# Norm offset parts on GpSimd behind the rotary tables' copies, and one row's attention norm offset on VectorE

## The chip, the cores and the metric

The kernel runs on one core of a Trainium2 chip, as one launch. The core's engines each work through their own fixed list of instructions: TensorE (PE in the profile, with PEld for the loading of weights), VectorE (DVE), ScalarE (ACT), GpSimd (POOL) and SyncE (SP, which only starts transfers here). Transfers are also started from GpSimd's list. An instruction waits at the head of its list until what it reads is there, and everything behind it on that engine waits too. The metric is device time in microseconds (us); lower is better.

## The reference

A decoder trunk of two layers over 1024 tokens of width 1024, all in float32. What matters here is the first layer's mixer and the norm behind it:

```
h = x @ w_in                                  # split: c_q (256), k, v (128 each), k_idx (128), w_idx (8)
k = apply_rope(k, cos_q, sin_q)               # 2 heads of 64, the first 16 elements rotate
k_idx = apply_rope(layer_norm(k_idx, g, b), cos_i, sin_i)     # the first 32 of 128 rotate
q, q_idx = apply_rope(c_q @ w_uq), apply_rope(c_q @ w_iq)
score = sum over 8 heads of w_idx * relu(q_idx . k_idx); keep the 256 best keys of each query
h = layer_norm(alpha * x + attention(q, k, v) @ w_o, ln_g, ln_b)
ffn = (silu(h @ w_gate) * (h @ w_up)) @ w_down
h = layer_norm(alpha * h + ffn, ...)          # and the same again with a gated recurrence as the mixer
```

`cos` and `sin` come from the positions; `layer_norm` is `(x - mean) * rsqrt(var + eps) * g + b`, and `b` is what is called the norm's offset below.

## The kernel before, in words

The 1024 tokens are 8 rows of 128 tokens (one row is 128 partitions x 1024 values; row 7 is the last). Every float32 product is made of three TensorE matmuls on a high and a low part of each operand (`mm3`, lines 110 to 112); ScalarE makes the high part by a cast, VectorE the low part by a subtraction.

**Attention's projections** (`att_in`). The steps in `ORDER_IN` are called one by one: `p0` projects row 0 with `w_in`, `f2` turns row 2 into feature order, `k0` makes the keys of rows 0 and 1, `w` splits the query weights, `q2` makes the queries of row 2, `s2` stores them, `a` advances the index scores. A scheduler then sets the order on each engine from the order of the calls and from what depends on what; the result is a fixed list for each engine.

Three things in this part matter here.

- **Rotary tables** (`rope_tables`). VectorE reduces the angles; ScalarE takes the sine twice (line 206, once for the cosine with a shift of a quarter turn); behind each sine GpSimd copies the table into a second half (line 207) and into a short table for the 64-wide heads (line 209, twice). `keys` (from line 1308) reads the short tables in its first rotary multiplication (line 221, tile `rk`). What follows there: two sums (lines 224, 225), ScalarE's split of the keys (line 1328, tile `kk`), and TensorE's transposes of the keys (line 1343).
- **Offset parts** (`kits`). For the later norms that are folded into matmuls, GpSimd prepares the offsets of two norms, each plain (`o...`) and multiplied by alpha (`p...`): a small 4-row tile `za` is loaded from memory (line 396), combined (lines 399 to 401), and split into three bfloat16 parts (lines 404, 408), each written back to memory (line 405). Before these, a 0/1 selector is made from the identity (line 388) and written three times (line 390). `kits` is a generator: each `next` emits one stretch of this work. Its results are read by `picks` and `parts` in the later down projections.
- **Index loads** (line 1441). While queries are stored, GpSimd's list also starts the loads of stored index queries (tile `it`), which TensorE multiplies with the index keys (tile `C`, from `kih`). On GpSimd's list they stand behind all of `kits`.

**The end of attention** (`att_main`). Rows 0 to 5 are normed while the last queries are attended; rows 6 and 7 at the very end by `layer_norm((6, 7), ...)`. For each row VectorE subtracts the mean and multiplies by the gain (line 151), ScalarE multiplies by the inverse deviation (line 152), and GpSimd adds the offset in two halves of 512 (line 154). The feed-forward's operands are then made of pairs of rows, (0, 2), (1, 3), (4, 6), (5, 7): `row_sums` subtracts rows of a pair (lines 374, 375, tile `gb`; on VectorE for the last two pairs), TensorE transposes rows and differences (line 352, tile `Y`), ScalarE and VectorE split them (lines 471, 472, tile `x`), and TensorE multiplies them with the first weights (tile `M`).

The calls at the point of the change are:

```
kits = self.kits(ap, self.tile(s.sel, [P, T], F32, "za"), s.bs)
for step in self.ORDER_IN.split():
    next(kits, None)
    does[step[0]](int(step[1:] or 0))
```

Of the kernel before, what the change touches and what calls it, by code (L numbers as in the profile page):

```python
# [18 lines left out]
ALU = mybir.AluOpType  # L19
# [48 lines left out]
class Core:  # L68
# [66 lines left out]
    def layer_norm(self, ts, g, b):  # L135

        nc, v = self.nc, self.nc.vector
        n = len(ts)
        mv = self.tile(self.small, [P, 4, 2], F32, "lnmv")[:, :n]
        for i, t in enumerate(ts):  # L140
            r = self.resid[:, t, :]
            st = self.tile(self.small, [P, 2, 6], F32, "lnst")
            for c in range(2):
                v.bn_stats(st[:, c, :], r[:, c * 512 : (c + 1) * 512])
            v.bn_aggr(mv[:, i, :], st.rearrange("p a b -> p (a b)"))
            yield
        rs = self.rsqrt(mv[:, :, 1], n, 1.0, LN_EPS, "ln")
        yield
        for i, t in enumerate(ts):
            r = self.resid[:, t, :]  # L150
            v.scalar_tensor_tensor(r, r, mv[:, i, 0:1], g, op0=ALU.subtract, op1=ALU.mult)
            nc.scalar.activation(r, r, AF.Copy, scale=rs[:, i : i + 1])
            for c in (slice(0, 512), slice(512, D)):
                nc.gpsimd.tensor_tensor(r[:, c], r[:, c], b[:, c], op=ALU.add)
            yield

    def row(self):
# [10 lines left out]
    def rope_tables(self, cp, wp, pt, it):  # L168

        nc, v = self.nc, self.nc.vector  # L170
        n = NT * 16
        pf = self.tile(wp, [P, NT], F32, "posf")
        v.tensor_copy(pf, pt)
        three = self.tile(wp, [P, 3, n], F32, "kk")
        ang, a1, a2 = (three[:, i, :] for i in range(3))
        v.tensor_tensor(
            ang.rearrange("p (t j) -> p t j", t=NT),
            pf.rearrange("p (t o) -> p t o", o=1).to_broadcast([P, NT, 16]),
            it.rearrange("p (o j) -> p o j", o=1).to_broadcast([P, NT, 16]),
            op=ALU.mult,  # L180
        )
        v.tensor_copy(a1.bitcast(F32R), ang)
        v.tensor_tensor(a2, ang, a1, op=ALU.subtract)
        turns = self.tile(wp, [P, 7, n], F32, "q")
        near = self.tile(wp, [P, 7, n], F32, "qi")
        for i, (a, p) in enumerate(((a1, 3), (a2, 2), (a1, 2), (a2, 1), (a1, 1), (a2, 0), (a1, 0))):
            v.tensor_scalar(turns[:, i, :], a, TURN[p], None, op0=ALU.mult)

        def frac(x, tmp, magic):
            v.tensor_scalar(tmp, x, magic, magic, op0=ALU.add, op1=ALU.subtract)  # L190
            v.tensor_tensor(x, x, tmp, op=ALU.subtract)

        frac(turns, near, 1.5 * 2.0**35)
        frac(turns, near, 1.5 * 2.0**23)
        u = turns[:, 0, :]
        for i in range(1, 7):
            v.tensor_tensor(u, u, turns[:, i, :], op=ALU.add)
        tabs = []
        for i, off in enumerate((0.25, 0.0)):
            w = turns[:, 1 + i, :]  # L200
            v.tensor_scalar(w, u, off, None, op0=ALU.add)
            frac(w, near[:, 0, :], 1.5 * 2.0**23)
            v.tensor_scalar(w, w, -0.4999999, 0.4999999, op0=ALU.max, op1=ALU.min)
            o, e = (self.tile(cp, [P, NT, 2, n], F32, f"rope{i}{n}") for n in (16, 8))
            w = w.rearrange("p (t j) -> p t j", t=NT)
            nc.scalar.activation(o[:, :, 0, :], w, AF.Sin, scale=2.0 * math.pi)
            nc.gpsimd.tensor_copy(o[:, :, 1, :], o[:, :, 0, :])
            for j in range(2):
                nc.gpsimd.tensor_copy(e[:, :, j, :], o[:, :, 0, 0:16:2])
            tabs.append((o, e))  # L210
        return zip(*tabs)

# [165 lines left out]
    def kits(self, pool, work, bs):  # L378

        nc, gp = self.nc, self.nc.gpsimd
        self.select = self.tile(self.kd, [12, 512], BF16, "select")
        self.kit = {}
        y = work[0:4, 0:256].bitcast(BF16)
        ones = self.ident[0:4, 0:4].rearrange("p (k o) -> p k o", o=1).to_broadcast([4, 4, P])
        gp.tensor_copy(y.rearrange("p (k c) -> p k c", k=4), ones)
        for j in range(3):
            gp.dma_start(self.select[4 * j : 4 * j + 4], y)  # L390
        yield
        rest, part = work[0:4, 0:512], work[0:4, 512:1024].bitcast(BF16)
        four = rest.rearrange("k (i c) -> k i c", i=4)
        for b, name, scale in bs:
            o = self.kit[name] = self.tile(self.kd, [12, 512], BF16, self.name(name[0]))
            gp.dma_start(four[:, 0:2, :], b.rearrange("(i k c) -> k i c", i=2, k=4))
            yield
            if scale is not None:
                gp.tensor_scalar(four[:, 0:2, :], four[:, 0:2, :], scale, None, op0=ALU.mult)
            gp.tensor_tensor(four[:, 2, :], four[:, 0, :], four[:, 1, :], op=ALU.subtract)  # L400
            gp.tensor_scalar(four[:, 3, :], four[:, 1, :], -1.0, None, op0=ALU.mult)
            for j in range(3):
                x = part[:, j % 2 * 512 : (j % 2 + 1) * 512]
                gp.tensor_copy(x, rest)
                gp.dma_start(o[4 * j : 4 * j + 4], x)
                yield
                if j < 2:
                    gp.tensor_tensor(rest, rest, x, op=ALU.subtract)
# [809 lines left out]
    def att_in(self, ap, csp, tp, x):  # L1218
        nc, v, gp, s = self.nc, self.nc.vector, self.nc.gpsimd, self.att
# [199 lines left out]

        does = dict(p=project, f=feature, k=keys, q=query, s=store, w=lambda _: query_weights(), a=lambda _: advance())  # L1420
        kits = self.kits(ap, self.tile(s.sel, [P, T], F32, "za"), s.bs)
        for step in self.ORDER_IN.split():
            next(kits, None)
            does[step[0]](int(step[1:] or 0))

    @staticmethod
# [608 lines left out]
```

## Time and profile before

| what | value |
|---|---|
| median of 3 runs | 2513.41 us (2510.82 to 2516.71) |
| the profiled execution | 2517.95 us |
| its span, first to last instruction | 2516.2 us |
| mean granted TensorE clock | 0.989 |
| TensorE busy | 2441.9 us |
| VectorE busy | 1906.9 us |
| ScalarE busy | 1056.2 us |
| GpSimd busy | 176.9 us |

The prediction quotes rows of the profile. A row of the timeline reads: start and duration in us, engine, line, operation, what is written from what, shapes, how many of a kind, and in brackets the engine's idle time ahead of it with what ended it. A row of the waits reads: engine, tile and line that waited, `<-` what it waited for: us in total, times, longest. A row of the windows reads: from and to, length, then busy time and number of instructions for PE, PEld, DVE, ACT and POOL, the granted TensorE clock as a share of full speed, the busy share of the transfer engines, and GB/s. A matmul of 128x384 has a moving operand of 384 columns. All times in rows are counted from the span's start.

### The profile page before, as it was taken

What the parts mean: (1) busy time and instruction counts of PE and PEld (TensorE: products, weight loads), DVE (VectorE), ACT (ScalarE), POOL (GpSimd) and SP (SyncE); (2) the same over time, 40 slices, a digit from 0 to 9 for tenths busy, and PEclk for the clock granted to TensorE, in tenths of its full rate; (3) what the DMA queues carried; (4) which work ended last, traced back from release to release, by engine and by line L of the source; (5) the groups of instructions that cost most, each with busy time, mean ns of one, the idle gap of its engine ahead of it and who ended that gap; (6) DMA issues with size and microseconds to landing.
All of it is one profiled execution on the core that took longest, in us unless ns stands there. A gap on an engine that the chain in (4) does not pass through costs nothing.

```text
span 2516.2 us, 35546 instructions
## 1 busy us (share of the span) xinstructions
PE 2441.9 (97%) x12810; PEld 2041.3 (81%) x12810; DVE 1906.9 (76%) x3692; ACT 1056.2 (42%) x1972; POOL 176.9 (7%) x295
## 2 busy tenths in 40 slices
PE   6998999999999999999999999999999999999998
PEld 6887888888888888888788888887778888888886
DVE  6578776788997766566898888887889867665767
ACT  4467666564333333334443333333353333333431
POOL 6001002000000000000011111111000000000000
PEclk8998999999999999999999999999999999999999
DMA  3337001011895332665431111113638733326853
GB/s 133 109 125 240 26 22 56 18 47 71 291 328 176 94 120 92 236 217 195 144 104 47 55 43 55 43 55 110 230 122 293 267 101 93 121 92 235 281 183 117
DMA packets 140127, 338.94 MB, mean 135 GB/s; under 512 B 17288, under 2 KB 18088, under 8 KB 132264
## 3 DMA queue, kind: packets, MB, share of 16 engines
q1 hardware_dynamic: 137224, 329.19, 38.6%
q0 software_dynamic: 2720, 7.42, 1.0%
q8 instruction: 101, 1.65, 0.3%
q14 instruction: 82, 0.67, 0.1%
HBM read 232.15 MB, written 104.39 MB: 134 GB/s over the span
## 4 chain that ended last, share of the span: by engine, by line
PE 64%; issue 10%; DVE 5%; DMA 2%; ACT 1%; POOL 1%; SPq 0%; DVEq 0%; ACTq 0%; POOLq 0%
PE Y L112 11%; PE Y L110 11%; PE Y L111 11%; PE M L111 8%; PE M L112 8%; PE M L110 7%; PE M L1082 3%; PE M L352 1%; DVE w L472 1%; DMA raw<-in_wd_dram 1%; PE M L1067 1%; PE M L1144 1%; PE M L1131 1%; PE M L1146 1%; PE M L354 0%
## 5 line engine op out<-in xcount | busy, mean ns | idle before, releaser
L471 ACT CAST w<-raw 128x512 fp32r<-128x512 f32 (+1 forms) x373 | 288.3, 775 | 527.7 <-PE Y L112 273.8
L472 DVE TENSOR_TENSOR w<-raw,w 128x512 fp32r<-128x512 f32 (+1 forms) x373 | 327.1, 881 | 180.8 <-ACT w L471 178.6
L110 PE MATMUL Y<-x,w 128*128 128x512 f32 (+1 forms) x1120 | 433.2, 387 | 1.8 <-DVE rows L789 0.7
L111 PE MATMUL Y<-x,w 128*128 128x512 f32 (+1 forms) x1120 | 429.9, 384 | 0.0
L112 PE MATMUL Y<-x,w 128*128 128x512 f32 (+1 forms) x1120 | 428.1, 382 | 0.0
L111 PE MATMUL M<-x,w 128*128 128x512 f32 (+1 forms) x644 | 245.7, 382 | 3.3 <-DVE x L472 3.3
L110 PE MATMUL M<-x,w 128*128 128x512 f32 (+1 forms) x644 | 245.6, 381 | 0.1
L110 PEld LDWEIGHTS Y<-x,w 128*128 128x128 f32 x1120 | 211.8, 189 | 41.3 <-ACT w L471 1.2
L112 PE MATMUL M<-x,w 128*128 128x512 f32 (+1 forms) x644 | 245.2, 381 | 0.0
L112 PEld LDWEIGHTS Y<-x,w 128*128 128x128 f32 x1120 | 211.8, 189 | 39.2 <-issue 0.9
L111 PEld LDWEIGHTS Y<-x,w 128*128 128x128 f32 x1120 | 211.9, 189 | 37.1 <-issue 0.2
L471 ACT CAST w<-s 128x512 fp32r<-128x512 f32 x180 | 111.8, 621 | 303.6 <-PE Y L112 116.5
L472 DVE TENSOR_TENSOR w<-s,w 128x512 fp32r<-128x512 f32 x180 | 124.4, 691 | 52.0 <-ACT w L471 51.1
L111 PEld LDWEIGHTS M<-x,w 128*128 128x128 f32 x644 | 121.6, 189 | 26.6 <-DVE x L472 3.7
L110 PEld LDWEIGHTS M<-x,w 128*128 128x128 f32 x644 | 121.5, 189 | 24.3 <-ACT x L471 1.2
L112 PEld LDWEIGHTS M<-x,w 128*128 128x128 f32 x644 | 121.6, 189 | 22.8
L110 PE MATMUL Y<-w 128*128 128x512 f32 x284 | 111.8, 394 | 0.2 <-ACT ph L471 0.2
L111 PE MATMUL Y<-w,w 128*128 128x512 f32 x284 | 111.4, 392 | 0.1
L112 PE MATMUL Y<-w,w 128*128 128x512 f32 x284 | 111.4, 392 | 0.0
L111 PE MATMUL M<-w,w 128*128 128x512 f32 x248 | 97.0, 391 | 1.3 <-DVE w L472 1.3
L112 PE MATMUL M<-w,w 128*128 128x512 f32 x248 | 96.9, 391 | 0.0
L110 PE MATMUL M<-w 128*128 128x512 f32 x248 | 96.1, 391 | 0.2 <-ACT ph L471 0.2
(497 smaller groups left out, 5112.4 us busy)
## 6 DMA issues: line engine op xcount, KB each, us to landing
raw<-in_wgu_dram SPq DMA_DIRECT2D x44, 1024.0 KB, 6.1
wdt<-in_wd_dram SPq DMA_DIRECT2D x44, 512.0 KB, 5.2
raw<-in_wd_dram SPq DMA_DIRECT2D x66, 256.0 KB, 4.2
raw<-in_hw_dram SPq DMA_DIRECT2D x16, 1024.0 KB, 4.8
qd<-qx SPq DMA_DIRECT2D x16, 512.0 KB, 3.6
qt<-qd SPq DMA_DIRECT2D x64, 128.0 KB, 2.7
t5q<-wdt SPq DMA_DIRECT2D x26, 256.0 KB, 3.7
t7q<-wdt SPq DMA_DIRECT2D x26, 256.0 KB, 2.7
```

Of the source, the lines that this page charges most:

```text
L110: mm(out, a[0], b[0], start=first, stop=False, **kw)
L111: mm(out, a[0], b[1], start=False, stop=False, **kw)
L112: mm(out, a[1], b[0], start=False, stop=last, **kw)
L352: mm(y[:, c], x[:, c], self.ident, **flags)
L471: self.nc.scalar.copy(hi, x)
L472: ins = (eng or self.nc.vector).tensor_tensor(lo, x, hi.bitcast(F32), op=ALU.subtract)
L1067: nc.tensor.matmul(pl[:, n, :], kk[:, m : m + P], y[:, n, :], start=True, stop=True)
L1082: nc.tensor.matmul(pl[rows, n, cols], lhs, rhs, start=True, stop=True)
L1131: nc.tensor.matmul(pd[:, n, :], kt[:, n, :], vt[:, n, :], start=True, stop=True)
L1144: nc.tensor.matmul(po[:, n, :], at[:, n, :], vt[:, n, :], start=True, stop=states[n] is None)
L1146: nc.tensor.matmul(po[:, n, :], qd[:, n * P : (n + 1) * P], states[n], start=False, stop=True)
```

## The change

Three edits.

- The `kits` generator is not advanced during the first six steps (`p0 f2 p1 f3 k0 w`); it starts at the seventh, `p2`.
- Its first instruction, the cast that makes the selector, gets an order-only dependence on the last copy of the rotary tables: on GpSimd's list it may not stand ahead of it.
- In `layer_norm` the two halves of row 7's offset are added by VectorE. Rows 6 and 7 are normed together by one call, and only attention's norm goes through this function; the other rows stay on GpSimd.

```diff
@@ layer_norm
             for c in (slice(0, 512), slice(512, D)):
-                nc.gpsimd.tensor_tensor(r[:, c], r[:, c], b[:, c], op=ALU.add)
+                (v if t == 7 else nc.gpsimd).tensor_tensor(r[:, c], r[:, c], b[:, c], op=ALU.add)
@@ rope_tables
             for j in range(2):
-                nc.gpsimd.tensor_copy(e[:, :, j, :], o[:, :, 0, 0:16:2])
+                self.roped = nc.gpsimd.tensor_copy(e[:, :, j, :], o[:, :, 0, 0:16:2])
@@ kits
-        gp.tensor_copy(y.rearrange("p (k c) -> p k c", k=4), ones)
+        self.behind(gp.tensor_copy(y.rearrange("p (k c) -> p k c", k=4), ones), self.roped)
@@ att_in
-        for step in self.ORDER_IN.split():
-            next(kits, None)
+        for i, step in enumerate(self.ORDER_IN.split()):
+            if i > 5:
+                next(kits, None)
             does[step[0]](int(step[1:] or 0))
```

`behind` adds a dependence that sets the order on the engine's list and no wait.

**GpSimd's list near the start.** Before, the tables' copies (tile `rope`; 76 and 77 belong to the cosine, 78 and 79 to the sine) stand inside the third offset, `o_131`:

```order
L396 DMA za_292<-in_lnb_dram 4x2x128
L400 TENSOR_TENSOR za_292<-za_292 4x128
L401 TENSOR_SCALAR za_292<-za_292 4x128
L404 CAST za_292<-za_292 4x512
L405 DMA o_131_682<-za_292 4x512
L207 COPY rope_76_276<-rope_76_276 128x8x16
L209 COPY rope_77_277<-rope_76_276 128x8x8 x2
L408 TENSOR_TENSOR za_292<-za_292 4x512
L404 CAST za_292<-za_292 4x512
L405 DMA o_131_682<-za_292 4x512
```

and the sine's copies six rows further on. With the change (line numbers from 1423 on are one higher):

```order
L1502 TENSOR_SCALAR marks_129<-marks_129 128x1
L1662 MEMSET bias_13_85 128x256
L1664 AFFINE_SELECT bias_14_86<-bias_14_86 128x128
L1664 AFFINE_SELECT bias_13_85<-bias_13_85 128x128
L207 COPY rope_76_276<-rope_76_276 128x8x16
L209 COPY rope_77_277<-rope_76_276 128x8x8 x2
L207 COPY rope_78_286<-rope_78_286 128x8x16
L209 COPY rope_79_287<-rope_78_286 128x8x8 x2
L388 CAST za_292<-ident 4x512
L390 DMA select_527<-za_292 4x512 x3
L396 DMA za_292<-in_lnb_dram 4x2x128
L400 TENSOR_TENSOR za_292<-za_292 4x128
```

All copies now stand ahead of the selector and the four offsets; the index loads of line 1441 still stand behind the last offset.

**VectorE's list at the end of attention.** Before, the pair sums (`gb_10624` for rows 4 and 6, `gb_10627` for rows 5 and 7) and the operands' low parts (tile `x`, from transposes in `Y`) stand so:

```order
L509 TENSOR_TENSOR raw_10412<-raw_10412,M_10516 128x256
L374 TENSOR_TENSOR gb_10624<-resid_2201 128x512
L375 TENSOR_TENSOR gb_10624<-gb_10624,resid_2201 128x512
L472 TENSOR_TENSOR x_1619_10380<-Y_10562,x_1619_10380 128x4x128
L374 TENSOR_TENSOR gb_10627<-resid_2201 128x512
L472 TENSOR_TENSOR x_1619_10380<-Y_10569,x_1619_10380 128x4x128
L472 TENSOR_TENSOR x_1620_10381<-Y_10589,x_1620_10381 128x4x128
L375 TENSOR_TENSOR gb_10627<-gb_10627,resid_2201 128x512
```

and with the change:

```order
L509 TENSOR_TENSOR raw_10412<-raw_10412,M_10516 128x256
L374 TENSOR_TENSOR gb_10624<-resid_2201 128x512
L154 TENSOR_TENSOR resid_2201<-resid_2201,gb_2236 128x512 x2
L472 TENSOR_TENSOR x_1619_10380<-Y_10562,x_1619_10380 128x4x128
L472 TENSOR_TENSOR x_1619_10380<-Y_10569,x_1619_10380 128x4x128
L375 TENSOR_TENSOR gb_10624<-gb_10624,resid_2201 128x512
L472 TENSOR_TENSOR x_1620_10381<-Y_10589,x_1620_10381 128x4x128
L374 TENSOR_TENSOR gb_10627<-resid_2201 128x512
L509 TENSOR_TENSOR raw_10412<-raw_10412,M_10445 128x256
L375 TENSOR_TENSOR gb_10627<-gb_10627,resid_2201 128x512
```

The second low part of `x_1619` moves ahead of both sums that follow the offset, and row 7's offset stands between the first sum and the first low part. On ScalarE's and SyncE's lists nothing moves; on TensorE's list one matmul of 128x256 passes the first four transposes of the sums.

## The prediction

> **What bounds the kernel now.** I read the page's busy shares first, then the waits of TensorE, then the windows around its longest wait. The rows are: the page's TensorE share, three of its waits (up to 640 us), and two windows.
>
> ```profile
> PE 2441.9 (97%) x12810; PEld 2041.3 (81%) x12810; DVE 1906.9 (76%) x3692; ACT 1056.2 (42%) x1972; POOL 176.9 (7%) x295
> ...
> PE C L1343 <- ACT kk L1328: 15.9, 1, 15.9
> ...
> PE C L110 <- DMA it<-id: 5.0, 4, 1.8
> PE M L111 <- DVE x L472: 3.3, 1, 3.3
> ...
> 40.00:50.00 10.00, 0.00 (x0) 0.00 (x0) 0.00 (x0) 0.00 (x0) 7.75 (x15) 0.51 0.01 2
> 50.00:60.00 10.00, 7.04 (x34) 6.76 (x35) 7.64 (x27) 3.38 (x11) 7.71 (x14) 0.64 0.01 1
> ```
>
> TensorE is busy for 97% of the span, and every list is fixed, so what TensorE idles is what can be won: an idle stretch that disappears moves everything behind it forward. The largest single one is 15.9 us, and in the window 40 to 50 only GpSimd works, while the transfer engines are at 0.01. This stall has one cause at a time, which the timeline around it shows, engine by engine:
>
> ```profile
> 36.07 0.33 PE L111 MATMUL A<-winl,xsh 128*128 128x384 f32 x1
> ...
> 38.82 0.31 ACT L206 ACTIVATE rope<-q 128x128 f32<-128x128 f32 x1 [3.95 <-DVE q L203]
> ...
> 39.81 0.16 DVE L123 SCALAR_TENSOR_TENSOR aiy<-ait,aiy 128x4 f32<-128x4 f32 x1
> ...
> 49.84 0.28 POOL L207 COPY rope<-rope 128x128 f32<-128x128 f32 x1
> 50.08 0.41 POOL L209 COPY rope<-rope 128x64 f32<-128x64 f32 x2
> ...
> 50.52 0.23 DVE L221 TENSOR_TENSOR rk<-hc,rope 128x64 f32<-128x64 f32 x1 [10.55 <-POOL rope L209]
> ...
> 51.56 0.71 ACT L1328 CAST kk<-hc 128x256 fp32r<-128x256 f32 x2 [12.11 <-DVE aiy L123]
> ...
> 52.33 1.97 PE L1343 MATMUL C<-ident,kk 128*128 128x128 f32 x8 [15.93 <-ACT kk L1328]
> ```
>
> The second sine is there at 39.13, its copies run only at 49.84 to 50.49, because they stand behind offset work on GpSimd's list. VectorE waits 10.55 us at its first rotary multiplication, and from that multiplication to the transposes of the keys it is another 1.8 us.
>
> **The change part by part. First term: the copies move ahead.** Were nothing else different, the copies (0.65 us) would end at 39.13 + 0.65 = 39.8 and the stall would shrink by 50.5 - 39.8 = 10.7 us. But the offset work also goes away from the stretch before the sine, and there it slows VectorE:
>
> ```profile
> 21.08 1.48 DVE L190 TENSOR_SCALAR qi<-q 128x896 f32<-128x896 f32 x1
> ...
> 24.50 0.61 DVE L190 TENSOR_SCALAR qi<-q 128x896 f32<-128x896 f32 x1
> ...
> 33.35 0.21 DVE L203 TENSOR_SCALAR q<-q 128x128 f32<-128x128 f32 x1
> ...
> 33.62 1.12 DVE L119 TENSOR_SCALAR aiy<-aih 128x4 int32<-128x4 int32 x1
> ...
> 37.62 1.17 DVE L203 TENSOR_SCALAR q<-q 128x128 f32<-128x128 f32 x1
> ...
> 66.39 0.16 DVE L119 TENSOR_SCALAR aiy<-aih 128x4 int32<-128x4 int32 x1
> ...
> 31.83 1.05 ACT L1256 CAST w_iqh<-sc 128x1024 fp32r<-128x1024 f32 x1 [1.70 <-DMA sc<-in_w_iq_dram]
> ...
> 34.41 0.46 ACT L1303 COPY hc<-A 128x384 f32<-128x384 f32 x1
> ```
>
> The same instruction on the same shape takes 1.48 or 0.61, 1.17 or 0.21, 1.12 or 0.16 us: 0.87 + 0.96 + 0.96 = 2.8 us too long in three instructions, and the long ones lie where GpSimd computes. So the sine could start at 38.82 - 2.8 = 36.0. With smaller stretches it may be earlier still, but not before ScalarE has ended its copy, 34.41 + 0.46 = 34.9, and that copy stands behind a cast that itself waited for a load, so GpSimd has no hand in it. I take 35.4, in the middle. Sine 0.3, copies 0.65: 36.4. The selector's cast now starts right behind the copies and may hold VectorE's multiplication for up to its 0.6 us (row below); half of that gives 36.7. Gain 50.5 - 36.7 = **13.8 us**. The lower end: VectorE stays as slow as it is, and the cast holds it fully, 10.7 - 0.6 = 10.1. The upper end: sine at 34.9, no hold, multiplication at 35.9, gain 14.6. TensorE is still busy to 36.4, so about 2 us of its idle time remain.
>
> **Second term: the clock behind the stall.** In the window 50 to 60 TensorE worked 7.04 us at a granted clock of 0.64. At full clock that is 4.5 us, 2.5 less. With a gap of 2 instead of 15.9 us the clock may stay up, but the transposes there also wait for VectorE's key chain, so I take **1.5**, with ends 0 and 2.5. The Trainium skill (TensorE: Matmul & The Clock Gate, Part 1) says that the clock is halved after an idle window of some 3.4 us, and restored after as long a busy one. By that rule a gap of 2 us costs no clock and the term is at its upper end. The two windows agree as far as the long gap goes (0.51, then 0.64); no row here has a gap of 2 us.
>
> **Third term: the offsets run later, beside other work.** All offset work of GpSimd, some 50 us, now starts at 36.7. What is queued behind it are the index loads:
>
> ```profile
> 2.71 0.60 POOL L388 CAST za<-ident 4x512 bf16<-4x512 f32 x1 [0.92 <-DMA ident<-in_ident_dram]
> ...
> 11.03 0.66 POOL L396 DMA_DIRECT2D za<-in_lnb_dram  x1 [4.53 <-DMA select<-za]
> ...
> 23.87 0.65 POOL L396 DMA_DIRECT2D za<-in_lnb_dram  x1
> ...
> 40.21 0.65 POOL L396 DMA_DIRECT2D za<-in_lnb_dram  x1
> ...
> 50.97 0.65 POOL L396 DMA_DIRECT2D za<-in_lnb_dram  x1
> ...
> 61.95 0.54 POOL L405 DMA_DIRECT2D p<-za  x1 [0.29 <-POOL za L404]
> ...
> 99.17 1.12 POOL L1441 DMA_DIRECT2D it<-id  x2 [36.68 <-DMA id<-qx]
> ...
> 109.32 0.42 PE L110 MATMUL C<-kih,it 128*128 128x384 f32 x1
> ...
> DMA to landing us min/median/max: 3.1/3.9/5.2
> ```
>
> The four offsets begin at 11.03, 23.87, 40.21 and 50.97, and the last ends at 62.5: 12.8, 16.3, 10.8 (9.5 without the two groups of copies) and 11.5 us; the selector takes 8.3 at most. The first two ran while VectorE was full and transfers dense, the last two while both were calmer, as they are from 37 on. So 2 x (9.5 + 11.5) plus about 5 for the selector, an estimate from these rows, is 47 us: the end at 83.7. TensorE first needs an index load at 109.3 - 15.3 = 94.0, and the load takes two issues and a median of 3.9 us, about 4.5: it must be issued by 89.5. There are 6 us to spare, so the wait costs nothing. What it does cost is VectorE's stretch in its key and query work from 62 us on, which was free of GpSimd:
>
> ```profile
> 57.37 1.00 DVE L221 TENSOR_TENSOR rk<-hc,rope 128x64 f32<-128x64 f32 x1
> ...
> 59.47 0.23 DVE L221 TENSOR_TENSOR rk<-hc,rope 128x64 f32<-128x64 f32 x1
> ```
>
> One rotary multiplication is 0.8 us longer beside GpSimd. Four or five such, each hidden in TensorE's queue for the most part, I price at **-1.0**, with ends 0 and -4 (five of 0.8 all on the path).
>
> **Fourth term: row 7's offset on VectorE.**
>
> ```profile
> 598.77 2.19 ACT L152 ACTIVATE resid<-resid,lny 128x1024 f32<-128x1024 f32 x2
> ...
> 600.00 2.53 POOL L154 TENSOR_TENSOR resid<-resid,gb 128x512 f32<-128x512 f32 x2 [74.52 <-ACT resid L152]
> ...
> 604.17 1.71 POOL L154 TENSOR_TENSOR resid<-resid,gb 128x512 f32<-128x512 f32 x1
> ...
> 601.34 1.75 DVE L374 TENSOR_TENSOR gb<-resid 128x512 f32<-128x512 f32 x1 [0.87 <-POOL resid L154]
> ...
> 605.92 0.69 DVE L374 TENSOR_TENSOR gb<-resid 128x512 f32<-128x512 f32 x1 [0.56 <-POOL resid L154]
> 606.53 0.68 DVE L472 TENSOR_TENSOR x<-Y,x 128x512 fp32r<-128x512 f32 x1
> ...
> 607.27 0.58 PE L111 MATMUL M<-x,w 128*128 128x256 f32 x1 [3.33 <-DVE x L472]
> ```
>
> TensorE stands for 3.33 us at an operand whose low part is queued behind the second pair's sum, and that sum waits for row 7's offset, which GpSimd ends at 605.88. With the change GpSimd is done with row 6 at 602.53. The first sum still runs against GpSimd's second half and ends at 603.1. Then VectorE: two halves of row 7 (ScalarE was ready at 600.96) and two low parts, four instructions 0.61 apart (as 605.92 and 606.53 are): 605.5. TensorE continues at 605.6 instead of 607.27: **1.7 us**. If the halves took GpSimd's 1.27 us each, only 0.4 would be left; if the first sum were not slowed, 2.8. The Trainium skill (SBUF — State Buffer, section "SBUF: two separate sides") calls the port pair of VectorE and GpSimd an exclusive lock, so that the loser waits for the whole instruction. The rows agree: the first sum ends 0.56 us behind the end of GpSimd's second half, and GpSimd's last half takes 1.71 instead of 1.27. The same rule speaks against the third term, since each offset instruction may then stop a rotary one; by it that term would be near its lower end.
>
> **Fifth term:** with the gap at 1.7 instead of 3.3 us the clock may stay up; I take **0.5**, ends 0 and 1.1 (the same share of the gap's 3.33 as 2.5 would be at most of 7.04).
>
> Sum: 13.8 + 1.5 - 1.0 + 1.7 + 0.5 = 16.5 us. Against its own time, the profiled execution of 2517.95 us (span 2516.2 and 1.75 around it) goes to 2501.5. That execution was 4.5 above the median of the runs; from the median, 2513.41 - 16.5 = **2497**. The ends of the terms, added: 10.1 + 0 - 4 + 0.4 + 0 = 6.5 and 14.6 + 2.5 + 0 + 2.8 + 1.1 = 21.0, thus 2492 to 2507.
>
> **The rivals.**
>
> *VectorE was not slowed by GpSimd.* The long rows above could have other causes, and the sine stays at 38.8. Then only the 10.1 of the first term holds: 16.5 - 3.7 = 12.8, time 2500.6. For it: the profile names no cause of a long instruction. Against it: equal instructions come out up to seven times apart in length, and the short L119 lies where GpSimd is idle. Chance 0.23.
>
> *The index loads become the wait.* If all four offsets take as long as the first two, 8.3 + 2 x (12.8 + 16.3) = 66.5, they end at 103.2, 13.7 us behind what TensorE needs; 2.8 us of the gain remain, time 2510.6. For it: the queue is in order, and the third term's stretch slows GpSimd too. Against it: the transfers are idle there (0.01 in two windows). Chance 0.03.
>
> *The same, further: slower.* All of the gain is gone when the offsets take 89.5 + 16.5 - 36.7 = 69.3 us; from there each us is a loss. If every offset took the longest, 16.3, it would be 73.5 us, 4.2 us too many: 2517.6. For it: GpSimd and VectorE now collide in the rotary work of the keys and queries. Against it: it asks for the slowest offset four times. Chance 0.03.
>
> *The gain is given back.* TensorE already waits 5.0 us for index loads; if transfers further on were paced by something other than the lists, the first three terms would vanish and 2.2 remain: 2511.2. Against it: no wait here hangs on a fixed time. Chance 0.03. That the copies do not move is ruled out by the lists; that they move and still wait is the first rival.
>
> **How the numbers follow.** My forecast has 0.68, the rivals 0.23, 0.03, 0.03 and 0.03. The range takes in the forecast's ends and the first rival, widened by some 2 us on the lower side for the spread of the runs shown (2510.82 to 2516.71) and by 1 above: 2490 to 2508. What a measurement of this kernel can tell from no change is about 0.2%, 5 us: faster means below 2508.4. Faster: 0.68 + 0.23 = 0.91; within 0.2%: 0.03 + 0.03 = 0.06; slower: 0.03.
>
> **What would show it.** Right: the wait of TensorE's key transposes falls from 15.9 to about 2 us, the second sine starts near 35.4, the rows 21.08 and 33.62 come back at 0.61 and 0.16, the window behind the stall has a clock near 1, the offsets end near 84 and the first index loads wait for the stored queries, not for GpSimd. At the end of attention TensorE's wait is near 1.7 us. Wrong: a sine still near 38.8 (first rival), index loads issued right behind an offset's last write (second and third), or a stall as short as forecast, with the start of the feed-forward part not earlier by about 17 us (fourth).

## The result, and the profile after

| | before | after |
|---|---|---|
| median | 2513.41 us (2510.82 to 2518.57, 5 runs) | 2498.80 us (2497.97 to 2501.23, 5 runs) |
| profiled execution | 2517.95 us, span 2516.2 | 2497.97 us, span 2496.2 |
| mean granted TensorE clock | 0.989 | 0.995 |

The ratio is 0.9941, with a 95% interval of 0.9926 to 0.9957: 14.8 us faster, between 10.8 and 18.6. The two profiled executions differ by 20.0 us, because that of before lay 4.5 above its median and that of after 0.8 below its own.

The page's busy shares of after, and TensorE's waits:

```profile
PE 2434.2 (98%) x12810; PEld 2033.9 (81%) x12810; DVE 1909.5 (76%) x3694; ACT 1057.1 (42%) x1972; POOL 171.6 (7%) x293
```

```profile
PE C L110 <- DMA it<-id: 4.6, 4, 1.8
...
PE B L1396 <- DVE qx L230: 3.3, 1, 3.3
...
PE C L1343 <- ACT kk L1328: 2.4, 1, 2.4
...
PE M L111 <- DVE x L472: 1.6, 1, 1.6
PE C L1354 <- DVE hc L225: 1.6, 1, 1.6
...
PE C L1343 <- DVE xsl L230: 0.8, 1, 0.8
```

The wait at the key transposes fell from 15.9 to 2.4 us and that at row 7 from 3.3 to 1.6. Three waits on VectorE are new or longer: 0.8 at the transposes of the second keys, 1.6 at the sums `hc` behind them, 3.3 at the queries' low part `qx` (before had two there, the longer one 1.2). The stretch behind the stall, in windows:

```profile
40.00:50.00 10.00, 9.41 (x67) 8.37 (x65) 9.15 (x28) 6.23 (x17) 6.52 (x10) 1.00 0.22 66
50.00:60.00 10.00, 7.91 (x56) 7.37 (x57) 8.59 (x26) 2.50 (x7) 7.13 (x11) 1.00 0.12 46
...
80.00:90.00 10.00, 6.65 (x37) 6.23 (x36) 8.07 (x20) 2.15 (x4) 4.75 (x8) 0.83 0.29 111
```

Where before stood still from 40 to 50 and ran at a clock of 0.64 from 50 to 60, TensorE now works at full clock. From 80 to 90 it idles for 3.35 us and its clock is 0.83; in before the same work lies some 11 us later, and from 90 to 100 TensorE there has 9.65 us of work and a clock of 1.00.

The timeline around the tables (VectorE's once long instructions, the sine, the selector's cast, the first rotary multiplication, the key transposes):

```profile
20.62 0.63 DVE L190 TENSOR_SCALAR qi<-q 128x896 f32<-128x896 f32 x1
...
32.83 0.17 DVE L119 TENSOR_SCALAR aiy<-aih 128x4 int32<-128x4 int32 x1
...
35.44 0.22 DVE L203 TENSOR_SCALAR q<-q 128x128 f32<-128x128 f32 x1
...
35.70 0.31 ACT L206 ACTIVATE rope<-q 128x128 f32<-128x128 f32 x1 [0.55 <-DVE q L203]
...
36.73 0.60 POOL L388 CAST za<-ident 4x512 bf16<-4x512 f32 x1
36.82 0.60 DVE L221 TENSOR_TENSOR rk<-hc,rope 128x64 f32<-128x64 f32 x1 [0.18 <-POOL rope L209]
...
39.00 1.15 PE L1343 MATMUL C<-ident,kk 128*128 128x128 f32 x8 [2.44 <-ACT kk L1328]
```

The three VectorE instructions that took 1.48, 1.12 and 1.17 us before take 0.63, 0.17 and 0.22. The sine starts at 35.70 and the multiplication at 36.82, where the selector's cast holds it (0.60 instead of the 0.23 of before).

**Where the gain arises and where it is lost.** The two lists of TensorE hold the same 12810 matmuls, so each can be followed: the table gives by how much the same instruction starts earlier than in the profile of before.

| TensorE instruction (its start before) | change | change again |
|---|---|---|
| key transposes (52.33) | 13.3 | 14.3 |
| next key transposes, L1354 (59.52) | 16.0 | 15.7 |
| L1354 of the second keys (72.55) | 13.8 | 13.6 |
| query transposes, L1396 (96.30) | 10.8 | 10.5 |
| first index product (109.32) | 10.8 | 10.4 |
| at 300 | 13.6 | 10.7 |
| ahead of the wait at row 7 (600.1) | 13.7 | 10.8 |
| behind that wait (607.27) | 15.4 | 12.5 |
| at 613 | 16.1 | 13.2 |
| at 1000 | 16.1 | 11.2 |
| last | 20.0 | 14.0 |

The right column is a second profile of the same kernel. Up to the index products the two agree within 1 us; from 300 to 613 they stand 3 us apart, at 1000 it is 5, and at the end 6. So up to the index products and across row 7 the columns tell something, and a difference of a few us late in the span does not. Much of this drift can be the clock: the second profile has 41.4 us at half clock, the first 27.4 (before 58.0), and if TensorE worked through all of the 14.0 us between them, they cost 7.0 us (an estimate). Both lose 5.2 or 5.3 us between the second and the fourth line. The rows of that stretch, GpSimd's and VectorE's side by side:

```profile
47.15 0.69 POOL L404 CAST za<-za 4x512 bf16<-4x512 f32 x1
...
47.29 0.68 DVE L230 TENSOR_TENSOR xsl<-C,xsh 128x512 fp32r<-128x512 f32 x1
...
57.40 1.14 POOL L408 TENSOR_TENSOR za<-za 4x512 f32<-4x512 f32 x1
57.44 1.15 DVE L225 TENSOR_TENSOR hc<-hc,rk 128x32 f32<-128x32 f32 x1
...
58.73 0.41 PE L1354 MATMUL C<-ident,hc 128*128 128x128 f32 x2 [1.58 <-DVE hc L225]
...
78.83 1.23 POOL L408 TENSOR_TENSOR za<-za 4x512 f32<-4x512 f32 x1
78.97 1.39 DVE L221 TENSOR_TENSOR rq<-xin,rope 128x256 f32<-128x256 f32 x1
...
81.66 1.19 POOL L408 TENSOR_TENSOR za<-za 4x512 f32<-4x512 f32 x1
81.76 1.24 DVE L225 TENSOR_TENSOR xin<-xin,rq 128x128 f32<-128x128 f32 x1
...
83.80 0.54 POOL L405 DMA_DIRECT2D p<-za  x1 [0.29 <-POOL za L404]
85.51 1.12 PE L1396 MATMUL B<-ident,q 128*128 128x128 f32 x4 [3.35 <-DVE qx L230]
88.39 1.13 POOL L1442 DMA_DIRECT2D it<-id  x2 [4.04 <-DMA id<-qx]
...
98.50 0.43 PE L110 MATMUL C<-kih,it 128*128 128x384 f32 x1
```

The long VectorE rows at 57.44, 78.97 and 81.76 each end just behind the end of a GpSimd sum on a tile of only 4 partitions: 57.40 + 1.14 = 58.54 against 58.59, 78.83 + 1.23 = 80.06 against 80.36, 81.66 + 1.19 = 82.85 against 83.00. Without company these three take 0.18, 0.42 and 0.29 us in the profile of before. What they lose stays in VectorE's list: its instruction at 74.86 (88.67 before) is 13.8 us ahead of before, the queries' low part at 84.77 (95.56 before) only 10.8. TensorE then stands 1.58 us at the key sums (58.73), where before has no wait, and 3.35 us at the transposes behind the queries' low part (85.51), where before had 0.35. The rows of before:

```profile
72.22 0.18 DVE L225 TENSOR_TENSOR hc<-hc,rk 128x32 f32<-128x32 f32 x1
...
92.31 0.42 DVE L221 TENSOR_TENSOR rq<-xin,rope 128x256 f32<-128x256 f32 x1
...
93.84 0.29 DVE L225 TENSOR_TENSOR xin<-xin,rq 128x128 f32<-128x128 f32 x1
...
96.30 0.66 PE L1396 MATMUL B<-ident,q 128*128 128x128 f32 x4 [0.35 <-DVE qx L230]
```

The index loads, which the rivals feared for, wait for the stored queries (4.04 us), long after GpSimd's last write at 83.80.

The end of attention:

```profile
586.33 2.54 POOL L154 TENSOR_TENSOR resid<-resid,gb 128x512 f32<-128x512 f32 x2 [74.45 <-ACT resid L152]
...
587.66 1.75 DVE L374 TENSOR_TENSOR gb<-resid 128x512 f32<-128x512 f32 x1 [0.87 <-POOL resid L154]
...
589.34 1.28 DVE L154 TENSOR_TENSOR resid<-resid,gb 128x512 f32<-128x512 f32 x2
...
591.87 0.39 PE L111 MATMUL M<-x,w 128*128 128x256 f32 x1 [1.61 <-DVE x L472]
```

Row 7's two halves take VectorE 0.60 us each (the low part behind them starts at 590.54), as assumed; the first pair's sum still runs against GpSimd's second half of row 6 (1.75).

### The profile page after: what moved, and what is told of

It is laid out like the page before. It is cut to its first block, busy times and chain, and to the rows that moved or that the text cites. A ratio compares the mean times of both kernels' runs of the same rounds, so it can differ in the third digit from the quotient of the medians.

```text
span 2496.2 us, 35544 instructions
## 1 busy us (share of the span) xinstructions
PE 2434.2 (98%) x12810; PEld 2033.9 (81%) x12810; DVE 1909.5 (76%) x3694; ACT 1057.1 (42%) x1972; POOL 171.6 (7%) x293
## 4 chain that ended last, share of the span: by engine, by line
PE 79%; DVE 5%; issue 4%; ACT 1%; DMA 1%; POOL 0%; SPq 0%; DVEq 0%; ACTq 0%; POOLq 0%
PE Y L112 12%; PE Y L110 12%; PE Y L111 12%; PE M L111 8%; PE M L110 8%; PE M L112 8%; PE M L1082 3%; PE O L1846 3%; PE L L1875 2%; PE O L1789 1%; PE M L352 1%; PE T L1841 1%; PE M L1067 1%; DVE w L472 1%; PE W L112 1%
```

## The experiments

Two things had to be told apart. Is the total the sum of its two halves, or is something given back? And what took the 5.2 us between 59 and 96: GpSimd's arithmetic beside VectorE (my reading of the rows above), or the offsets' transfers and their place in GpSimd's queue? The kernels came in three sets, each on one chip with its own runs of before: (1) e1, e2, e3, e5 beside 15 runs of before, median 2515.04; (2) e4, e6, e7, e8 beside 11, 2514.61; (3) e9, e10 beside 11, 2515.99.

| kernel | median, us | ratio to before, 95% interval |
|---|---|---|
| e1 offsets only | 2504.51 | 0.9954 (0.9941 to 0.9968) |
| e2 row 7 only | 2513.48 | 0.9989 (0.9980 to 0.9998) |
| e3 offsets behind the index loads | 2498.03 | 0.9929 (0.9915 to 0.9942) |
| e5 light offsets | 2494.62 | 0.9916 (0.9903 to 0.9930) |
| e8 the change again | 2503.72 | 0.9948 (0.9935 to 0.9961) |
| e4 first offset ahead | 2501.71 | 0.9942 (0.9929 to 0.9955) |
| e6 rows 6 and 7 on VectorE | 2499.91 | 0.9941 (0.9928 to 0.9953) |
| e7 offsets made together | 2495.41 | 0.9927 (0.9914 to 0.9939) |
| e10 the same again | 2497.23 | 0.9919 (0.9905 to 0.9934) |
| e9 together, rows 6 and 7 on VectorE | 2495.87 | 0.9913 (0.9898 to 0.9928) |

All diffs are against the change; `...` marks lines left out.

### Each half by itself: e1 and e2

e1 leaves row 7's offset on GpSimd:

```diff
-                (v if t == 7 else nc.gpsimd).tensor_tensor(r[:, c], r[:, c], b[:, c], op=ALU.add)
+                nc.gpsimd.tensor_tensor(r[:, c], r[:, c], b[:, c], op=ALU.add)
```

> Only the offset parts behind the copies; row 7's offset stays on GpSimd. My theory (the parts add): TensorE's wait at the key transposes falls from 15.93 to about 2.4 us, the index products start about 10.8 us earlier than before (98.5 instead of 109.3), the operand behind row 7 about 13.7 us earlier and with the old wait of about 3.3 us; the time is 13 to 14 us below before, near 2500, and some 2 us above the full change. Rival (the row 7 edit carries more than its own wait, for what follows is paced by transfers that start there): the gain behind the feed-forward's first operands falls by more than 3 us against the full change.

e2 keeps only row 7's edit:

```diff
-                self.roped = nc.gpsimd.tensor_copy(e[:, :, j, :], o[:, :, 0, 0:16:2])
+                nc.gpsimd.tensor_copy(e[:, :, j, :], o[:, :, 0, 0:16:2])
...
-        self.behind(gp.tensor_copy(y.rearrange("p (k c) -> p k c", k=4), ones), self.roped)
+        gp.tensor_copy(y.rearrange("p (k c) -> p k c", k=4), ones)
...
-        for i, step in enumerate(self.ORDER_IN.split()):
-            if i > 5:
-                next(kits, None)
+        for step in self.ORDER_IN.split():
+            next(kits, None)
             does[step[0]](int(step[1:] or 0))
```

> Only row 7's offset on VectorE; the offset parts stay where they were. My theory: nothing changes up to the end of attention, the wait of 3.33 us there falls to about 1.6 us, and with the clock kept up the gain behind it is 2.0 to 2.6 us: about 2511 us, which the runs cannot tell from no change. Rival (the wait shrinks only because the first edit moved the phase of something): the wait stays near 3 us.

TensorE's waits of e1, then of e2:

```profile
PE M L111 <- DVE x L472: 3.3, 1, 3.3
PE C L1343 <- ACT kk L1328: 2.2, 1, 2.2
```

```profile
PE C L1343 <- ACT kk L1328: 16.5, 1, 16.5
...
PE M L111 <- DVE x L472: 1.6, 1, 1.6
```

Each half removes its own wait and leaves the other's. The ratios give 0.46% and 0.11%, together 0.57%, against 0.59% measured for both (0.52% the second time): within the intervals the halves add, and nothing of the one is given back by the other. Across row 7's wait e2 gains 1.7 us (from 1.4 behind to 0.3 ahead of before's instruction) and 0.7 more by 613, which it has lost again at 640 (0.3 ahead); e1 gains nothing there. e1 loses the same 5.3 us between 59 and 96 as the change, 16.7 to 11.5, so the loss belongs to the offsets. Its 11.6 us by the ratio are less than the 13 to 14 expected, which the interval (8 to 15 us) still takes in.

### The loss beside the keys and queries: e3, e4, e5

e3 puts all offset work behind the last of the early index loads, so GpSimd is idle beside keys and queries:

```diff
-        self.behind(gp.tensor_copy(y.rearrange("p (k c) -> p k c", k=4), ones), self.roped)
+        self.behind(gp.tensor_copy(y.rearrange("p (k c) -> p k c", k=4), ones), self.att.loaded)
...
-            if i > 5:
+            if i > 28:
                 next(kits, None)
...
-            s.fetch.dma_start(it.bitcast(F32), s.ids[j][:, k])
+            s.loaded = s.fetch.dma_start(it.bitcast(F32), s.ids[j][:, k])
```

> The full change, but the offset parts are put behind the last early index load (they run from about 120 us on, beside the index scores) instead of behind the copies. My theory (GpSimd's offset work slows VectorE in the key and query work and costs what the trace shows given back, 16.0 at the second key transposes to 10.8 us at the index products): the gain stays near 16 us, at least 15, up to the index products; behind 120 us part of it is lost, 1 to 4 us, so that the time is between 2495 and 2500. Rival (the 5 us are given back by transfers or by the order on TensorE, which this kernel leaves as it is): the gain at the index products is again 10 to 11.5 us.

e5 keeps the place of the offsets, their loads and writes, but has one cast for each instead of seven or eight instructions; it leaves out the sums and the scaling, so its offsets aren't the reference's:

```diff
-            if scale is not None:
-                gp.tensor_scalar(four[:, 0:2, :], four[:, 0:2, :], scale, None, op0=ALU.mult)
-            gp.tensor_tensor(four[:, 2, :], four[:, 0, :], four[:, 1, :], op=ALU.subtract)
-            gp.tensor_scalar(four[:, 3, :], four[:, 1, :], -1.0, None, op0=ALU.mult)
+            half = rest[:, 0:256].rearrange("k (o c) -> k o c", o=1).to_broadcast([4, 2, 256])
+            x = part[:, 0:512]
+            gp.tensor_copy(x.rearrange("k (o c) -> k o c", o=2), half)
             for j in range(3):
-                x = part[:, j % 2 * 512 : (j % 2 + 1) * 512]
-                gp.tensor_copy(x, rest)
                 gp.dma_start(o[4 * j : 4 * j + 4], x)
                 yield
-                if j < 2:
-                    gp.tensor_tensor(rest, rest, x, op=ALU.subtract)
```

> The full change, but of each offset only one cast and the writes are left on GpSimd; the sums, the scaling and the split into three parts are left out, so the later norms' offsets are not the reference's. GpSimd's compute instructions between 37 and 90 us fall from 31 to 5, its transfers stay. My theory (the port shared by GpSimd and VectorE): the gain at the index products rises from 10.8 to 14.5 to 16 us and stays, the time is 3 to 5 us below the full change. Rival (transfers from GpSimd's queue or the order on TensorE): it stays at 10 to 11.5 us.

e4 makes the selector and the first offset at the start, as before did, and the other three behind the copies:

```diff
-        self.behind(gp.tensor_copy(y.rearrange("p (k c) -> p k c", k=4), ones), self.roped)
+        gp.tensor_copy(y.rearrange("p (k c) -> p k c", k=4), ones)
...
-            gp.dma_start(four[:, 0:2, :], b.rearrange("(i k c) -> k i c", i=2, k=4))
+            ins = gp.dma_start(four[:, 0:2, :], b.rearrange("(i k c) -> k i c", i=2, k=4))
+            if name != bs[0][1]:
+                self.behind(ins, self.roped)
...
-            if i > 5:
+            if i != 5:
                 next(kits, None)
```

> The full change, but the selector and the first offset run at the start, as before the change, and only the other three offsets stand behind the copies. My theory (what costs is how long GpSimd computes beside VectorE's key and query work): VectorE's long rows come back between 15 and 24 us (the angle's reduction at about 1.5 instead of 0.6 us), but ScalarE's cast that waits for a load hides most of it, so the key transposes are 12.5 to 13.5 us earlier than before; the three offsets end near 71 instead of 84 us, and the gain at the index products is 12 to 14 us instead of 10.8. Rival (the loss is fixed as soon as any offset runs there): it stays at 10 to 11.5 us.

By how much the same TensorE instruction starts earlier than before:

| instruction (start before) | change | e4 | e3 | e5 |
|---|---|---|---|---|
| key transposes (52.33) | 13.3 | 12.8 | 13.2 | 14.7 |
| next key transposes (59.52) | 16.0 | 14.5 | 15.8 | 17.4 |
| second keys (72.55) | 13.8 | 12.2 | 16.5 | 17.7 |
| query transposes (96.30) | 10.8 | 12.2 | 16.5 | 17.7 |
| first index product (109.32) | 10.8 | 12.0 | 16.4 | 17.8 |

The query transposes and the first index product in the trace of e3, then a write and a key sum in that of e5:

```profile
79.76 0.66 PE L1396 MATMUL B<-ident,q 128*128 128x128 f32 x4 [0.34 <-DVE qx L230]
...
92.89 0.43 PE L110 MATMUL C<-kih,it 128*128 128x384 f32 x1
```

```profile
53.37 1.57 POOL L402 DMA_DIRECT2D o<-za  x3 [0.29 <-POOL za L400]
...
54.50 0.18 DVE L225 TENSOR_TENSOR hc<-hc,rk 128x32 f32<-128x32 f32 x1
```

With no offset work there (e3) the loss is gone, and the 3.35 us wait is 0.34 again. With its transfers all issued and only the arithmetic cut (e5), it is gone just as well. At the keys that speaks against the transfers: e5's sum at 54.50 takes its usual 0.18 us beside three writes. At the queries e5 alone decides nothing, for its last write is out at 59.45; there the change's own rows do, where a sum of VectorE at 81.56 takes 0.28 us beside the write that GpSimd issues from 81.11 to 81.65, and the next one 1.24 beside the sum behind it. So GpSimd's arithmetic is the cause, not its transfers. That e5 stands at 17.8 and not at the 14.5 to 16 expected comes in part from ahead of the loss: it is 1.4 us further than the change at the key transposes already. e4, whose last offset ends at 70.0, ahead of the queries, loses its part at the keys alone: 2.5 instead of 5.2, and nothing between 72 and 96.

What e3 wins is partly paid later. Its offset work then runs beside the index scores, where an instruction that starts at 145.69 us with the change starts at 141.62. Its lead over the change has fallen from 5.6 us at the index products to 4.1 there, and to 1.6 at 300 us (the last within what two profiles of one kernel differ by). By the runs it is 0.9929, and the change 0.9941 and 0.9948: these intervals overlap, so that e3 beats the change isn't shown. For e5 against e1 (same set, 0.9916 and 0.9954, of which row 7 explains 0.0011) 0.0027 remain, 6.8 us, about what the traces show at the index products (17.8 against e1's 11.4). e4 costs some of the gain at the tables too, 1.5 us at 59.52 (14.5 against 16.0), and by its runs cannot be told from the change. I had expected the loss at the tables in a VectorE row beside the first offset, and it isn't there:

```profile
22.89 0.63 DVE L190 TENSOR_SCALAR qi<-q 128x896 f32<-128x896 f32 x1
```

The offset's arithmetic had just ended ahead of it. The loss shows instead at a key sum for which the next key transposes wait (0.95 us), held by a sum of the second offset, which begins sooner here:

```profile
43.70 1.15 DVE L225 TENSOR_TENSOR hc<-hc,rk 128x32 f32<-128x32 f32 x1
...
45.00 0.41 PE L1356 MATMUL C<-ident,hc 128*128 128x128 f32 x2 [0.95 <-DVE hc L225]
```

### Both rows of the last pair: e6

```diff
-                (v if t == 7 else nc.gpsimd).tensor_tensor(r[:, c], r[:, c], b[:, c], op=ALU.add)
+                (v if t > 5 else nc.gpsimd).tensor_tensor(r[:, c], r[:, c], b[:, c], op=ALU.add)
```

> The full change, and row 6's offset on VectorE too. My theory (VectorE's first pair sum is held for one whole GpSimd half, 587.66 to 589.4 in the changed kernel): without GpSimd there the operand's low part is ready about 1 us earlier, TensorE's wait of 1.61 us falls to 0.3 to 0.8 us; the time is 1 us lower, which the runs cannot tell. Rival (the pair sum takes 1.75 us of its own): VectorE gets 1.3 us more work and the wait grows to 2 us or more.

VectorE's rows of the four halves and of the first pair's sum in e6:

```profile
587.30 2.50 DVE L154 TENSOR_TENSOR resid<-resid,gb 128x512 f32<-128x512 f32 x4 [0.36 <-ACT resid L152]
...
592.65 0.68 DVE L374 TENSOR_TENSOR gb<-resid 128x512 f32<-128x512 f32 x1
```

Without GpSimd the sum takes 0.68 instead of 1.75 us, and TensorE's matmul no longer waits for the low part (the transposes behind it wait 1.1 us in all, 0.8 in the change). In e6's list the low parts, from 590.05 on, also stand ahead of that sum, so the shorter sum and the new order aren't told apart. Across that place its gain over before rises by 3.5 us (12.7 to 16.2), in the change by 1.7. TensorE's order differs from there to 621; at 625, behind it, e6 has gained 4.4 us and the change 2.5, so another 1.9 us are there in the trace. The runs (0.9941 against 0.9948 for e8 in the same set) are too coarse for it.

### The change again: e8

> The full change once more, on the same chip as the next three, as their measure. Both theories: 13 to 17 us below before, gain at the index products 10 to 12 us.

The ratio, 0.9948, agrees with 0.9941, and the trace with the first up to the index products, as the table above shows. One thing differs. TensorE's wait at the key transposes is 2.21 us here, no longer than the 2.44 of the first profile, and yet the clock fell behind it:

```profile
38.05 1.15 PE L1343 MATMUL C<-ident,kk 128*128 128x128 f32 x8 [2.21 <-ACT kk L1328]
...
39.39 0.51 PE L111 MATMUL A<-winl,xsh 128*128 128x384 f32 x1
```

In the first profile the matmuls of that shape behind the wait are at full pace:

```profile
40.16 0.34 PE L110 MATMUL A<-winh,xsh 128*128 128x384 f32 x1
```

It is 0.34 us there and 0.51 here. From the key transposes to the next the gain rises by 1.4 us here and by 2.7 in the first profile.

### The offsets made together: e7, e10, e9

If GpSimd's arithmetic costs by being there beside VectorE, the same offsets in fewer instructions must cost less. e7 lays both norms' offsets out on 32 partitions of 128 and makes plain and scaled at once: behind the tables seven instructions instead of thirty, with ten loads at the start and twelve writes.

```diff
+        plain, less, both = work[0:32, 0:128], work[0:32, 128:256], work[0:32, 256:512]
+        gp.memset(work[0:32, 0:256], 0.0)
+        for m, (b, _, _) in enumerate(bs[::2]):
+            rows = b.rearrange("(i k c) -> i k c", i=2, k=4)
+            for x, i, h in ((plain, 0, 0), (plain, 1, 1), (plain, 2, 0), (less, 2, 1), (less, 3, 1)):
+                gp.dma_start(x[16 * m + i : 16 * m + 16 : 4, :], rows[h])
+        yield
+        self.behind(gp.tensor_tensor(both[:, 0:128], plain, less, op=ALU.subtract), self.roped)
+        gp.tensor_scalar(both[:, 128:256], both[:, 0:128], ALPHA, None, op0=ALU.mult)
...
+        for j in range(3):
+            x = work[0:32, 768 + j % 2 * 128 : 896 + j % 2 * 128].bitcast(BF16)
+            gp.tensor_copy(x, both)
...
+            if j < 2:
+                gp.tensor_tensor(both, both, x, op=ALU.subtract)
```

> The full change, with the offset parts made differently: the values of both norms lie on 32 partitions with 128 values each instead of 4 with 512, all four offsets are made together, so that GpSimd's compute instructions for them fall from 31 to 9, each on 128 to 512 values per partition; the results are the same up to rounding. My theory (shared port): like the kernel with the light offsets, the gain at the index products is 15 to 17.5 us, and the time 4 to 6 us below the full change, near 2494. Rival (what counts is the number of GpSimd's transfers, here 25 instead of 19): no better than the full change.

A sum and the last write of GpSimd, then TensorE's query transposes and first index product, in e7:

```profile
41.82 0.68 POOL L412 TENSOR_TENSOR za<-za 32x256 f32<-32x256 f32 x1
...
48.21 0.48 POOL L409 DMA_DIRECT2D p<-za  x1
```

```profile
79.32 0.66 PE L1400 MATMUL B<-ident,q 128*128 128x128 f32 x4 [0.34 <-DVE qx L230]
...
92.79 0.41 PE L110 MATMUL C<-kih,it 128*128 128x384 f32 x1
```

A sum over 256 elements on 32 partitions takes 0.68 us, over 512 on 4 partitions 1.15: the length goes by the elements of a partition. All offset work is over at 48.7 instead of 84.3, and nothing is lost between 59 and 96 (16.3, then 17.0 at the query transposes). Whether it is the smaller number of instructions or their earlier end that counts isn't separated by this kernel; that no sum of GpSimd beside the second keys and the queries means no loss is what e3, e5 and e7 have in common.

e9 is e7 with rows 6 and 7 on VectorE, and e10 is e7 once more.

> The batched kernel a second time, beside the one with rows 6 and 7 on VectorE. By the theory its ratio to before is 0.992 to 0.9935 and its time near 2496, with the index products' first at 92 to 93.5 us; by the rival (the batched kernel's lead over the change came from one favourable set of runs) the ratio is 0.994 or more, the change's own, and the time 2499 to 2504.

> The batched offsets of both norms and, with them, the attention norm offsets of rows 6 and 7 on VectorE. By the theory (GpSimd's offset work costs by its count of instructions beside VectorE; a lone wait of TensorE is worth its own length and the clock behind it): the wait on VectorE for the x low part at row 7, 1.6 us in the batched kernel, is not listed, the first index product stands near 98.5 - 5.7 = 92.8 us as in the batched kernel, and the time is 1 to 2.5 us under the batched one's, near 2494. By the rival (row 6's offset on VectorE only takes the place of other VectorE work and the wait comes back elsewhere): the same wait is gone, another of 1.5 us or more is listed at TensorE between 560 and 620 us, and the time is 2496 to 2499.

e10 gives 0.9919 and e7 0.9927, the change 0.9941 and 0.9948. The means lie 0.0022 apart, 5.4 us; each mean is known to some 0.001 (two intervals of about 0.0014, taken as independent), so the lead is shown, if narrowly. At the first index product e10 stands 15.2 us ahead of before and e9 14.8, against 16.5 in e7: less than was expected. Some 0.9 us of that is there at the key transposes already (13.2 and 13.3 against 14.2), where ScalarE's second sine waits 1.38 us for VectorE. Another 0.7 comes behind them, where in both the clock fell after a wait of 2.8 and 3.0 us, here e9's:

```profile
39.00 1.34 PE L1347 MATMUL C<-ident,kk 128*128 128x128 f32 x8 [2.96 <-ACT kk L1332]
...
40.46 0.52 PE L110 MATMUL A<-winh,xsh 128*128 128x384 f32 x1
```

In e9 the matmul's wait at the x low part isn't listed, no other of its size takes its place, and its gain rises by 3.5 us across it (14.0 to 17.4), as in e6. The median, 1.4 us under that of e10, has the sign that was expected, but no set of runs here tells 1.4 us. Of the kernels that leave nothing out, e9 has the lowest ratio of this study, 0.9913.

## Why the prediction was right

The forecast was 2497 us in a range of 2490 to 2508; measured were 2498.8 and, in the second set, 2503.7. The main mechanism and the sign were right, but the total, 16.5 us forecast against some 14.8 and 13.1 (0.9948) measured, comes from errors that partly cancel, and that they do is luck.

- **First term, 13.8:** 13.3 and 14.3 measured at the key transposes in two profiles. The sine starts at 35.70 (35.4 was forecast), the multiplication at 36.82 (36.7), and VectorE's long rows came back short, which refutes the first rival. The cast of the selector holds the multiplication wholly; I had put in half of it.
- **Second term, 1.5, ends 0 and 2.5:** 2.7 where the clock stayed up (2.44 us of wait) and 1.4 where it fell (2.21). The value was a fair one, but for another reason than mine: it lies between two outcomes, and which of them comes isn't settled by the length of the wait (last section).
- **Third term, -1.0, end -4: this is the step that failed.** It cost 5.2 us. I priced "four or five" rotary instructions 0.8 us longer, hidden for the most part. The runs show that the held instructions lie ahead of TensorE's own operands: the key sums (wait of 1.58) and then the queries' low part (3.35). Neither was hidden. The clock that fell behind the second wait (0.83 in the window) cost nothing more: the lead is 10.8 us at the query transposes and at the first index product alike. The mechanism was the right one and was even named, but I took the size from one row of before instead of from the thirty instructions that moved (held were 1.39 for 0.42, 1.24 for 0.29, 1.15 for 0.18, 1.16 for 0.17 at line 118, and more). The timing itself was good: the offsets ended at 84.3 (83.7 was forecast), and the index loads waited for the stored queries, so the second and the third rival fall.
- **Fourth term, 1.7, and fifth, 0.5:** 1.71 and 0.75, twice (change and e2). Behind its 3.33 us before runs at half clock from 606.72 to 610.13; behind the change's 1.61 us the clock stays at 1.00.
- **Gain given back:** e1 and e2 add up, and the lead at the index products (10.8 and 10.4) isn't lost afterwards, so the fourth rival falls.

The terms as measured in the first profile are 13.3 + 2.7 - 5.2 + 1.7 + 0.75 = 13.3 us. That this is less than the 14.8 of the runs lies within their interval (10.8 to 18.6). The rest of the 16.1 us that this profile shows at 613 comes between 109 and 600, where the second profile gains 0.4 and not 2.9: it belongs to the drift and not to the change.

The Trainium skill (SBUF — State Buffer, section "SBUF: two separate sides") makes a VectorE operation with two SBUF inputs wait for the whole of a GpSimd operation that reads SBUF and started first. The rows agree in the held sums above, and also in the exception: the subtraction at 47.29, one of whose inputs (`C`) lies in TensorE's accumulator, takes its usual 0.68 us beside the cast at 47.15. The prediction had read that rule as a reason for the lower end of the third term, and still took a value near the upper.

## What to carry to other kernels

When work is moved away from one stall, list what runs on the neighbouring engine where it lands, and follow each of those instructions to the operand that TensorE wants next; "hidden in the queue" has to be read from TensorE's slack there, not assumed. How long a small helper computation on GpSimd lasted here went by how many instructions it has and how many elements each has on a partition, not by the partitions: spreading 4 partitions of 512 over 32 of 256, merging four passes into one and so ending it ahead of the second keys was worth about 5 us, more than a third of the change's whole gain. Where one profile shows a late difference of a few us, compare the time at half clock and take a second profile of the same kernel before explaining it. Price the clock behind a wait of 2 to 4 us as a chance (an estimate from the waits of the next section).

## What was not expected of the hardware

- **The clock behind a short wait.** At the key transposes, in kernels nearly alike up to there, the clock stayed at 1.00 after waits of 1.14 (e5), 1.35 (e7), 1.93 (e3), 2.17 (e1, e4), 2.44 (the change) and 2.65 us (e6), and fell to half after 2.21 (e8), 2.80 (e10) and 2.96 (e9). The length of the wait alone doesn't decide. What does at this place can be read from the traces. In each, the stretches of half clock last 3.41 us or a multiple and start whole multiples of 3.413 us apart (e8: 39.38 and 87.17, 14 x 3.413), as on a grid of steps that lies differently in every execution. The table has the most that TensorE idled, in this wait, within one step of the grid:

| kernel | wait, us | most of it in one step, us | clock in the next step |
|---|---|---|---|
| e5, e7, e3 | 1.14, 1.35, 1.93 | 0.90, 0.70, 1.03 | 1.00 |
| e4, e6 | 2.17, 2.65 | 1.17, 1.48 | 1.00 |
| the change, e1 | 2.44, 2.17 | 1.87, 1.89 | 1.00 |
| e8 | 2.21 | 2.08 | 0.50 |
| e10, e9 | 2.80, 2.96 | 2.45, 2.60 | 0.50 |

So one border between 1.89 and 2.08 us of idle time in a step fits all ten. The 2.44 us of the change fall into two steps (0.57 up to 37.12, 1.87 behind), the 2.21 of e8 almost whole into one (35.97 to 39.38). Elsewhere in the traces that border doesn't hold: in before the clock also fell behind a step with 1.07 us idle (up to 214.18), so what else counts stays open. The Trainium skill (TensorE: Matmul & The Clock Gate, Part 1) says that the window in which activity is watched runs freely, without regard to the program: that fits the grid. It also puts that window at some 3.4 us and asks for an idle one; in e8 TensorE worked 1.33 us of the step ahead of the fall, so there the trace differs from the page.
- **A sum on 4 partitions holds VectorE like one on 128.** The 0.18 us sum at 57.44 took 1.15 beside it, and at line 118 even a 128x4 instruction of 0.17 us took 1.16.
- **GpSimd is held too.** The copies of line 209 that take 0.41 us in the change's first profile take some 1.64 in e1, e3, e6, e9 and e10, in e3 from 34.90 to 36.54, beside a weight subtraction of VectorE from 34.90 to 36.11. They lie ahead of the second table's copies and so on the way to the key transposes, but cost nothing there in e3: the second sine, which waits for VectorE too, ends only at 36.59.
